# Convolution's means two iterations behind their power, the last gate's modulation fetched in pairs, the opening's blocks rounded ahead of the next columns

## The chip, the core and the metric

The kernel runs on one core of a Trainium2 chip, in one launch. The metric is the device time in microseconds; of several runs the median stands. The engines are TensorE (PE; its weight loads are listed apart as PEld), VectorE (DVE), ScalarE (ACT), GpSimd (POOL) and SyncE (SP), which issues most of the DMAs.

## What is computed

One encoder layer on x of 1024 x 1024 in float32, with three residual sub-layers: a SwiGLU FFN at half weight, a token mixer (a convolution group beside differential attention), and a second FFN. Each sub-layer is

```
shift, scale, gate = mod[:, 0], mod[:, 1], mod[:, 2]       # mod = silu(c) @ w_ada + b_ada, 9 x 1024 columns
y = f(x * (1 + scale) + shift)
x = layer_norm(ALPHA * x + weight * (1 + gate) * y, g, b)
```

The convolution group ends in a layer norm over its 512 channels and a silu. Only three places of this matter here: the modulation of the first sub-layer, with which everything begins; that layer norm's means; and the gate of the last sub-layer.

## The kernel before

Products are made in float32r: each operand is split into a rounded part (a copy on ScalarE, L143) and a remainder (a subtraction on VectorE, L144), and a product is three matmuls (high by high, high by low, low by high). The FFN's products follow a Strassen scheme with seven products per pair of column blocks.

The order of the instructions on an engine is not simply the written order: a planner fills each engine's queue ahead of the run, and `tc.issue_after(ins)` ties what is written inside it behind `ins`, in the queue of the engine of `ins` alone. A tied instruction doesn't wait for `ins` to end, it only stands behind it. Once made, the queues are fixed, and an engine that waits at one instruction holds up all behind it. Large temporary blocks come from one heap of 30 slots (`slot`, L64; `raw_slot`, L201).

**The opening** (`early`, L767, with `first_ada`, `first_x`, `first_mod`, `first_h`, L705 to L763). The shift and scale columns of the first sub-layer come in four chunks kk of 256 columns each. A chunk's modulation weights are four loads q of two slices each, so 8 slices j of 128 x 512. `first_mod` sums the first 6 slices on VectorE (L729, L731; NV is 3, and the loop runs to 2 n), lets TensorE sum the other two by matmuls with one output column (L737, 16 passes), and adds up the 128 partitions by further matmuls (L747). ScalarE makes the columns B0 and A0 from these (L744, L751). `first_h` transposes the chunk's x block on TensorE (L759) and applies scale and shift on ScalarE (L255). `right_first` (L258) then splits that block. What stands in `issue_after(columns)` is tied behind the last column sum of the chunk before, on TensorE; what stands in `issue_after(summed)` behind the last sum on VectorE. The split of block kk - 1 is written behind the columns of chunk kk. `in_gate` and `in_sums` prepare the first weights of the FFN: the first at kk = 1, the sums at kk = 3. After the opening, `mid` (L794) starts the products, tied behind the last columns on TensorE, and handles the second half of x (L811 is its first step on VectorE).

**The convolution's means** (`conv_stat`, L1243). After four blocks' statistics GpSimd makes the reciprocal root by a power (L1246, L1248); some steps later VectorE makes the negative mean times it (L1252) and ScalarE normalizes the four blocks (L1255). The steps are counted by `step(ST)`, called once in each of the 32 iterations of the attention loop with ST = 5; a `yield` uses one. `finish` (L1213) does the like for the attention's norm, with 2 ST yields between its power (L1217) and its use (L1220). Chains stand in one list, and a chain begins when the one ahead of it has ended.

**The last gate** (`ada_gate`, L187, called from `hook2`, L1471). `hook2(j)` is called after the products of column block j of the last FFN. At j = 10 and 13 it fetches four slices of two for one half of the gate (L166), which also sums them on VectorE (L155, L157), tied to nothing there; two iterations later the rest is written (one matmul, L194, and L196, L197). `pace["Y"]` is the last weight load issued, `pace["V"]` the last product on VectorE of an iteration (L480).

Of the kernel before, what the change touches and what calls it, by code (L numbers as in the profile page):

```python
# [1 line left out]

# [6 lines left out]
F32 = mybir.dt.float32  # L10
# [3 lines left out]
ALU = mybir.AluOpType  # L14
# [3 lines left out]
P = 128  # L18
T = 1024
NT = T // P  # L20
D = 1024
KD = D // P
# [3 lines left out]
H = 512  # L26
# [14 lines left out]
ST = 5  # L41
# [1 line left out]
CF = 3  # L43
AHEAD = 4
LATE = 0
NV = (3, 3, 3, 3)

# [1 line left out]
def layer_kernel(ctx, tc, a, out):  # L51
    nc = tc.nc
    V, S, G, PE, SY = nc.vector, nc.scalar, nc.gpsimd, nc.tensor, nc.sync
# [10 lines left out]
    def slot(name, shape=(P, 2, H), dt=F32R):  # L64
        return heap.tile(list(shape), dt, tag="h", bufs=HEAP, name=name)

    def bank(name, dt=F32):
        return psum.tile([P, H], dt, tag="ps", bufs=4, name=name)
# [78 lines left out]

    w_ada = a["w_ada"][0].rearrange("(p j) n -> p j n", j=KD)

    def ada_acc(raws, acc):  # L150
        n = 0
        for raw in raws:
            for jj in range(raw.shape[1]):
                if n == 0:
                    V.tensor_scalar(acc, raw[:, jj], c_act[:, 0:1], None, ALU.mult)  # L155
                else:
                    V.scalar_tensor_tensor(acc, raw[:, jj], c_act[:, n : n + 1], acc, ALU.mult, ALU.add)  # L157
                n += 1

    def ada_chunk(wp, take, s, m, half):  # L160
        col = (s * 3 + m) * D + half * H
        acc = wp.tile([P, H], F32, tag="ada_acc", bufs=1, name=f"ada{s}{m}{half}")
        raws = []
        for q in range(4):
            raw = take(f"adaw{s}{m}{half}{q}")
            SY.dma_start(raw, w_ada[:, 2 * q : 2 * q + 2, col : col + H])  # L166
            raws.append(raw)
        ada_acc(raws, acc)
        return acc

    mods = {}
# [12 lines left out]

        return rest

    def ada_gate(wp, take, s, w, g, half):  # L187
        if half == 0:
            SY.dma_start(g, a["b_ada"][:, (s * 3 + 2) * D : (s * 3 + 3) * D].partition_broadcast(P))
        acc = ada_chunk(wp, take, s, 2, half)  # L190

        def rest():
            ps = bank(f"adag{s}{half}")
            PE.matmul(ps, lhsT=ones, rhs=acc, start=True, stop=True)  # L194
            sl = g[:, half * H : (half + 1) * H]
            V.tensor_scalar(sl, sl, w, w, ALU.mult, ALU.add)  # L196
            V.scalar_tensor_tensor(sl, ps, w, sl, ALU.mult, ALU.add)  # L197

        return rest

    def raw_slot(name):  # L201
        return slot(name, dt=F32)
# [55 lines left out]
    def right_first(name, ops, hb, eng=V):  # L258

        hi, lo = slot(f"{name}bh"), slot(f"{name}bl")  # L260
        last = split(hi, lo, hb, eng)
        ops["B11"].append((hi[:, 0], lo[:, 0]))
        ops["B21"].append((hi[:, 1], lo[:, 1]))
        return last
# [114 lines left out]
    pace = {}  # L379
# [316 lines left out]
    with pool("p1a") as wp:  # L696
        in_tags(wp, "r4 ah al mw sh sl")
        ops = new_ops()
# [23 lines left out]
        def first_mod(kk, raws, n):  # L722

            ps = bank(f"ada0p{kk}")
            acc = slot(f"ada0a{kk}", (P, 2, 2, 256), F32)[:, 0]
            for j in range(2 * n):
                raw = raws[j // 2][:, j % 2]
                if j == 0:
                    V.tensor_scalar(acc, raw, c_act[:, 0:1], None, ALU.mult)  # L729
                else:  # L730
                    last = V.scalar_tensor_tensor(acc, raw, c_act[:, j : j + 1], acc, ALU.mult, ALU.add)  # L731
            part = small.tile([P, 4], F32, tag="part", bufs=2, name=f"part{kk}")
            two = bank(f"ada0q{kk}")
            for i in range(4):
                m, es, k = i // 2, slice(i % 2 * P, (i % 2 + 1) * P), 2 * kk + i % 2
                for j in range(2 * n, KD):
                    PE.matmul(  # L737
                        two[:, i : i + 1], lhsT=raws[j // 2][:, j % 2, m, es], rhs=c_act[:, j : j + 1],
                        start=j == 2 * n, stop=j == KD - 1,
                    )  # L740
            for i in range(4):
                k = 2 * kk + i % 2
                bias = (bcol(0, 0), bada1)[i // 2]
                S.activation(part[:, i : i + 1], two[:, i : i + 1], AF.Identity, bias=bias[:, k : k + 1], scale=1.0)  # L744
            for i in range(4):
                m, es = i // 2, slice(i % 2 * P, (i % 2 + 1) * P)
                pe = PE.matmul(ps[:, i : i + 1], lhsT=acc[:, m, es], rhs=ones[:, 0:1], start=True, stop=True)  # L747
            for i in range(4):
                k = 2 * kk + i % 2
                to = (B0, A0)[i // 2]  # L750
                S.activation(to[:, k : k + 1], ps[:, i : i + 1], AF.Identity, bias=part[:, i : i + 1], scale=1.0)  # L751
            return last.ins, pe.ins

        def first_h(kk, x, half):
            ps = wide(f"hT0_{kk}_{half}")
            for e in range(2):
                for i in range(4):
                    o = e * H + i * P
                    flipped[:] = [PE.transpose(ps[:, o : o + P], x[:, i, e * P : (e + 1) * P], ident).ins]  # L759
            h = slot(f"h0_{kk}_{half}", dt=F32)  # L760
            for e in range(2):
                h_of(h[:, e], ps[:, e * H : (e + 1) * H], A0, B0, 2 * kk + e)
            return h  # L763
# [3 lines left out]
        def early(wp, s, w_in, ops):  # L767

            with tc.issue_after(c_silu.ins):
                raws = [in_load(wp, s, w_in, 0, S)]  # L770
            ada, xb = [], []
            for kk in range(4):
                ada.append(first_ada(kk))
                xb.append(first_x(kk, 0))
            xc = [first_x(kk, 1) for kk in range(2)]
            raws.append(in_load(wp, s, w_in, 1))
            xc.extend(first_x(kk, 1) for kk in range(2, 4))
            hb, L = [], [{}, {}]
            for kk in range(4):
                with tc.issue_after(columns) if kk else nullcontext():  # L780
                    summed, columns = first_mod(kk, ada[kk], NV[kk])
                    hb.append(first_h(kk, xb[kk], 0))
                with tc.issue_after(summed):
                    if kk:
                        right_first(f"r0_{kk - 1}", ops, hb[kk - 1])
                    if kk == 1:
                        L[0].update(in_gate(wp, s, 0, raws[0]))
                    if kk == 3:
                        right_first("r0_3", ops, hb[3])
                        in_sums(wp, s, 0, raws[0], L[0])  # L790
            first.update(wp=wp, s=s, w_in=w_in, ops=ops, hb=hb, xc=xc, L=L, raws=raws, pe=columns)
            return L, ({}, {}), mid

# [176 lines left out]
    with pool("mproj") as wp:  # L970
        us, sig = [], []
        for i in range(4):
            ws = (pre, pre2)[i] if i < 2 else load_glu(wp, i, "whi", "wlo", 4, "raw", 3)
            q = quad(f"glu{i}", i % 2)
            for hs in ((0,), (1,)) if i == 0 else ((0, 1),):
                for k in range(KD):
                    wh, wl = (w[:, k % 4] for w in ws[k // 4])
                    for n, (w, x) in enumerate(((wh, 0), (wh, 1), (wl, 0))):
                        for m in range(2):
                            for h in hs:  # L980
                                PE.matmul(  # L981
                                    q[2 * m + h], lhsT=w[:, m * P : (m + 1) * P], rhs=hm[k][h][:, x],
                                    start=k == 0 and n == 0, stop=k == KD - 1 and n == 2,
# [177 lines left out]
    with pool("mattn") as wp:  # L1161
# [81 lines left out]
        def conv_stat(half):  # L1243
            mv = cstat[half]
            v = small.tile([P, 4], F32, tag="cv", bufs=2, name=f"cv{half}")
            G.tensor_scalar(v, mv[:, :, 1], 1.0, EPS, ALU.mult, ALU.add)  # L1246
            r = small.tile([P, 4], F32, tag="cr", bufs=2, name=f"cr{half}")
            G.tensor_tensor(r, v, mhalf, ALU.pow)  # L1248
            for _ in range(ST):
                yield  # L1250
            nm = small.tile([P, 4], F32, tag="cnm", bufs=2, name=f"cnm{half}")
            V.scalar_tensor_tensor(nm, mv[:, :, 0], -1.0, r, ALU.mult, ALU.mult)  # L1252
            for t in range(4):
                blk = cacc[:, :, (4 * half + t) * P : (4 * half + t + 1) * P]
                S.activation(blk, blk, AF.Identity, bias=nm[:, t : t + 1], scale=r[:, t : t + 1])  # L1255
            cstat[half] = None
# [53 lines left out]
    ops = new_ops()  # L1310
    hb, hc = [None] * 4, [None] * 4
    todo2 = {}
    TENG = (V, G)
    with pool("p3a") as wp:
# [3 lines left out]
        for t in range(NT):  # L1318
            tag = ("sf", "sf", "sh", "sl", "sh", "sl", "sh", "sl")[t]
# [118 lines left out]
        for c in range(len(groups)):  # L1438
            last = c == len(groups) - 1
            for t in range(5 if last else NT):  # L1440
# [9 lines left out]
                if c == 1 and t == 0:  # L1450
                    raws = [in_load(wp, 2, a["ffn2_w_in"][0], j) for j in range(2)]
# [19 lines left out]
        def hook2(j):  # L1471
            if 1 < j < NT + 2:
                residual_tile(j - 2)
            if j in (10, 13):
                if j == 10:
                    mods["gate2"] = rows.tile([P, D], F32, tag="gate1", name="gate2")
                with tc.issue_after(pace["Y"]):
                    todo2[j + 2] = ada_gate(wp, raw_slot, 2, 0.5, mods["gate2"], (j - 10) // 3)
            if j in todo2:
                todo2.pop(j)()  # L1480

        def early2(wp, s, w_in, ops):
            return left, ({}, {}), mid
# [73 lines left out]
```

## Time and profile before

| | |
|---|---|
| median of 3 runs | 1894.91 us (1892.62 to 1895.3) |
| the profiled execution | 1899.15 us |
| its span | 1897.4 us |
| instructions | 23451 |
| granted TensorE clock, mean over the span | 0.99 |
| DMA | 288.73 MB, 152 GB/s over the span |

All times in views are microseconds from the span's start. In a timeline row stand the start, the length, the engine, the line of the kernel, the operation, output and inputs with their shapes, the count of instructions that the row merges, and in brackets how long the engine idled before and what released it. A queue name such as SPq stands for the issuing of DMAs. In a table by windows the numbers behind each engine are its busy time and, in parentheses, its instructions.

### The profile page before, as it was taken

The page shows a single profiled execution, that of the slowest core. Times are in us where ns is not written, and L with a number is a line of the kernel's source. Part 1 is how long each engine was busy: PE and PEld are TensorE (multiplying, and loading weights), DVE is VectorE, ACT ScalarE, POOL GpSimd, SP SyncE. Part 2 cuts the span into 40 slices and gives each one's busy share as a digit, 9 for nine tenths or more (in the row PEclk, how much of TensorE's full clock was granted, in tenths as well). Part 3 has the DMA queues.
Part 4 walks back from the last instruction along what each step waited for, and adds up shares of the span by engine and source line. Part 5 has one row for each costly group of instructions (what it writes and reads, how often), then busy time and mean ns, then how long its engine had stood idle before and what let it go on. Part 6 is the DMA issues. An engine that isn't in the chain of part 4 may idle for free. (4 is left out here: it accounts for less than half of the span.)

```text
span 1897.4 us, 23451 instructions
## 1 busy us (share of the span) xinstructions
PE 1826.3 (96%) x8570; PEld 1513.1 (80%) x8570; DVE 1439.1 (76%) x1979; ACT 784.9 (41%) x1292; POOL 317.4 (17%) x322
## 2 busy tenths in 40 slices
PE   5999999999999999999999899979999999999997
PEld 5787888887888887887888788758887888888885
DVE  4988877897688777999676566587776665469888
ACT  2643333333445543122277781453332333354540
POOL 0001111011200011036467540350000000000011
PEclk9999999999999999999999999989999999999999
DMA  9268867785894323222000134125554433187432
GB/s 319 72 225 281 257 228 239 242 268 189 301 322 131 100 60 134 83 95 70 20 1 1 45 134 134 78 83 183 167 166 152 145 120 106 45 293 275 135 113 72
DMA packets 219378, 288.73 MB, mean 152 GB/s; under 512 B 15978, under 2 KB 126687, under 8 KB 219262
## 3 DMA queue, kind: packets, MB, share of 16 engines
q1 hardware_dynamic: 204842, 245.25, 39.9%
q0 software_dynamic: 11072, 38.80, 5.6%
q10 hardware_dynamic: 3348, 3.18, 0.5%
q8 instruction: 67, 1.10, 0.2%
q14 instruction: 49, 0.40, 0.1%
HBM read 209.06 MB, written 78.12 MB: 151 GB/s over the span
## 5 line engine op out<-in xcount | busy, mean ns | idle before, releaser
L587 PE MATMUL fo<-wr,gl 128*128 128x512 f32 x1848 | 421.5, 390 | 1.0 <-DVE pv L630 1.0
L587 PEld LDWEIGHTS fo<-wr,gl 128*128 128x128 f32 x1848 | 346.3, 188 | 74.1 <-DVE pv L630 1.4
L1000 DVE SCALAR_TENSOR_TENSOR cacc<-u,convw,cacc 128x1012 f32<-128x1012 f32 (+14 forms) x120 | 150.9, 1322 | 0.2
L144 DVE TENSOR_TENSOR gl<-gr,gl 128x512 fp32r<-128x512 f32 x148 | 101.4, 691 | 12.5 <-ACT gl L143 11.0
L143 ACT CAST gl<-gr 128x512 fp32r<-128x512 f32 x148 | 90.8, 618 | 26.3 <-DMA gr<-gd 19.4
L144 DVE TENSOR_TENSOR sl<-sf,sh 128x1024 fp32r<-128x1024 f32 x43 | 54.5, 1267 | 59.0 <-ACT sh L143 58.9
L1131 DVE TENSOR_REDUCE mx<-sc 128x1 f32<-128x1024 f32 x64 | 75.5, 1215 | 26.2 <-PE sc L1129 26.0
L219 POOL TENSOR_TENSOR rr<-rv,mhalf 128x1 f32<-128x1 f32 x24 | 22.2, 925 | 431.4 <-DVE rv L217 431.4
L157 DVE SCALAR_TENSOR_TENSOR ada<-adaw,c_act,ada 128x512 f32<-128x512 f32 x98 | 73.2, 747 | 25.3 <-DMA adaw<-in_w_ada_dram 24.8
L143 ACT CAST sh<-sf 128x1024 fp32r<-128x1024 f32 x44 | 46.4, 1054 | 104.8 <-PE fi_16S L373 5.8
L1133 ACT ACTIVATE p<-sc,mx 128x1024 f32<-128x1024 f32 x64 | 71.4, 1117 | 36.1 <-DVE mx L1131 36.0
L395 POOL DMA_DIRECT2D gd<-gf x8 | 4.4, 546 | 413.6 <-DVE gf L461 412.5
L423 ACT ACTIVATE gf<-gf 128x512 f32<-128x512 f32 x44 | 27.8, 632 | 106.0 <-DVE gf L422 103.0
L143 ACT CAST wr<-wa 128x512 fp32r<-128x512 f32 x66 | 41.2, 624 | 71.1 <-PE fo L587 70.1
L443 ACT ACTIVATE gf<-gf 128x512 f32<-128x512 f32 x44 | 27.7, 629 | 98.8 <-DVE gf L442 98.8
L981 PE MATMUL glu<-hm,gluh 128*128 128x512 f32 x256 | 65.6, 392 | 0.0
L1182 POOL TENSOR_TENSOR p<-p,p 128x1024 f32<-128x1024 f32 x27 | 64.2, 2377 | 1.5
L143 ACT CAST wr<-wb 128x512 fp32r<-128x512 f32 x66 | 40.2, 621 | 57.5 <-PE fo L587 40.4
L144 DVE TENSOR_TENSOR wr<-wa,wr 128x512 fp32r<-128x512 f32 x66 | 45.4, 687 | 24.0 <-ACT wr L143 23.7
L1199 PE MATMUL av<-vf,aT 128*128 128x128 f32 x512 | 62.4, 276 | 1.0 <-ACT cacc L1262 1.0
L144 DVE TENSOR_TENSOR sl<-r,sh 128x1024 fp32r<-128x1024 f32 x44 | 53.6, 1221 | 11.8 <-ACT sh L143 11.7
L1199 PEld LDWEIGHTS av<-vf,aT 128*128 128x128 f32 x512 | 59.7, 192 | 1.5 <-ACT cacc L1262 1.3
(3436 smaller groups left out, 4874.1 us busy)
## 6 DMA issues: line engine op xcount, KB each, us to landing
gr<-gd SPq DMA_DIRECT2D x148, 256.0 KB
adaw<-in_w_ada_dram SPq DMA_DIRECT2D x56, 512.0 KB
gd<-gf SPq DMA_DIRECT2D x102, 256.0 KB
r<-in_ffn_w_in_dram SPq DMA_DIRECT2D x84, 256.0 KB
ra<-in_ffn_w_in_dram SPq DMA_DIRECT2D x66, 256.0 KB
mwi<-mw POOLq DMA_DIRECT2D x24, 512.0 KB, 5.9
wb<-in_ffn_w_out_dram SPq DMA_DIRECT2D x44, 256.0 KB
wa<-in_ffn_w_out_dram SPq DMA_DIRECT2D x44, 256.0 KB
```

Of the source, the lines that this page charges most:

```text
L143: a = S.copy(hi, x)
L144: b = eng.tensor_tensor(lo, x, hi.bitcast(F32), ALU.subtract)
L157: V.scalar_tensor_tensor(acc, raw[:, jj], c_act[:, n : n + 1], acc, ALU.mult, ALU.add)
L423: S.activation(c0, c0, AF.Silu)
L443: pace["S"] = S.activation(c1, c1, AF.Silu).ins
L587: PE.matmul(ps, lhsT=g[:, x, ts_], rhs=w[:, y], start=n in (1, 2, 3) and k == i == 0, stop=k == NK - 1 and i == 2, skip_group_check=n not ...
L981: PE.matmul(q[2 * m + h], lhsT=w[:, m * P : (m + 1) * P], rhs=hm[k][h][:, x], start=k == 0 and n == 0, stop=k == KD - 1 and n == 2,)
L1000: V.scalar_tensor_tensor(acc[:, lo_t:hi_t], u[:, lo_t + sh : hi_t + sh], convw[:, i, jj : jj + 1], acc[:, lo_t:hi_t], ALU.mult, ALU.add,)
L1131: V.tensor_reduce(mx_, ps, axis=AX.X, op=ALU.max, negate=True)
L1133: S.activation(pe, ps, AF.Exp, bias=mx_, accum_out=sm[:, e : e + 1])
L1182: last = G.tensor_tensor(p0, p0, p1, ALU.add)
L1199: PE.matmul(ps[:, 0:P], lhsT=aT[:, kt], rhs=vf[kt][:, h * P : (h + 1) * P], start=kt == 0, stop=kt == 7)
```

## The change

NV becomes 7 and `first_mod` counts slices with it instead of pairs, so VectorE sums 7 of 8 slices and TensorE one. In the opening the rounding of a block (the copy on ScalarE) is written right behind its `first_h`, and what the next chunk has on ScalarE is tied behind it; the remainder on VectorE stays tied behind the sums of the next chunk. The first weights' split is written at kk = 0 instead of 1, and their sums are halved: order 0 at kk = 1, order 1 at kk = 3. In `conv_stat` L1252 and L1255 are written 2 ST steps behind the power instead of ST. The last gate becomes a generator that `hook2` steps from j = 10 to 17: it fetches two slices (at 10 and 14), sums them an iteration later behind the product on VectorE and fetches the other two, sums these another iteration later, and writes the rest one iteration after that.

```diff
-NV = (3, 3, 3, 3)
+NV = (7, 7, 7, 7)
...
-    def ada_acc(raws, acc):
-        n = 0
+    def ada_acc(raws, acc, n=0):
...
-    def ada_gate(wp, take, s, w, g, half):
+    def ada_gate(wp, take, s, w, g, half, staged=False):
...
+        def slow():
+
+            col = (s * 3 + 2) * D + half * H
+            acc = wp.tile([P, H], F32, tag="ada_acc", bufs=1, name=f"ada{s}2{half}")
+            raws = {}
+
+            def fetch(q):
+                raws[q] = take(f"adaw{s}2{half}{q}")
+                SY.dma_start(raws[q], w_ada[:, 2 * q : 2 * q + 2, col : col + H])
+
+            with tc.issue_after(pace["Y"]):
+                fetch(0)
+                fetch(1)
+            yield
+            for n in (0, 2):
+                with tc.issue_after(pace["V"]):
+                    for q in (n, n + 1):
+                        ada_acc([raws[q]], acc, 2 * q)
+                if n == 0:
+                    with tc.issue_after(pace["Y"]):
+                        fetch(2)
+                        fetch(3)
+                    yield
+            yield
+            rest(acc)
...
-            for j in range(2 * n):
+            for j in range(n):
...
-                for j in range(2 * n, KD):
+                for j in range(n, KD):
                     PE.matmul(
                         two[:, i : i + 1], lhsT=raws[j // 2][:, j % 2, m, es], rhs=c_act[:, j : j + 1],
-                        start=j == 2 * n, stop=j == KD - 1,
+                        start=j == n, stop=j == KD - 1,
                     )
...
+            def right_lo(kk):
+                lo = slot(f"r0_{kk}bl")
+                V.tensor_tensor(lo, hb[kk], hi[kk].bitcast(F32), ALU.subtract)
+                ops["B11"].append((hi[kk][:, 0], lo[:, 0]))
+                ops["B21"].append((hi[kk][:, 1], lo[:, 1]))
+
+            hi = []
             for kk in range(4):
-                with tc.issue_after(columns) if kk else nullcontext():
+                with ExitStack() as es:
+                    if kk:
+                        es.enter_context(tc.issue_after(columns))
+                        es.enter_context(tc.issue_after(rounded))
                     summed, columns = first_mod(kk, ada[kk], NV[kk])
                     hb.append(first_h(kk, xb[kk], 0))
+                    hi.append(slot(f"r0_{kk}bh"))
+                    rounded = S.copy(hi[kk], hb[kk]).ins
                 with tc.issue_after(summed):
                     if kk:
-                        right_first(f"r0_{kk - 1}", ops, hb[kk - 1])
-                    if kk == 1:
+                        right_lo(kk - 1)
+                    if kk == 0:
                         L[0].update(in_gate(wp, s, 0, raws[0]))
-                    if kk == 3:
-                        right_first("r0_3", ops, hb[3])
-                        in_sums(wp, s, 0, raws[0], L[0])
+                    elif kk == 1:
+                        in_sums(wp, s, 0, raws[0], L[0], order=(0,))
+                    elif kk == 3:
+                        right_lo(3)
+                        in_sums(wp, s, 0, raws[0], L[0], order=(1,))
...
-            for _ in range(ST):
+            for _ in range(2 * ST):
                 yield
...
-            if j in (10, 13):
+            if j in (10, 14):
...
-                    todo2[j + 2] = ada_gate(wp, raw_slot, 2, 0.5, mods["gate2"], (j - 10) // 3)
-            if j in todo2:
-                todo2.pop(j)()
+                    todo2["gate"] = ada_gate(wp, raw_slot, 2, 0.5, mods["gate2"], (j - 10) // 4, staged=True)
+            if 10 <= j <= 17:
+                next(todo2["gate"], None)
```

## Rows read from the trace of the kernel before

**Rows 1.** The page, part 1: busy time, share and instructions of each engine.
```profile
PE 1826.3 (96%) x8570; PEld 1513.1 (80%) x8570; DVE 1439.1 (76%) x1979; ACT 784.9 (41%) x1292; POOL 317.4 (17%) x322
```

**Rows 2.** Waits of TensorE over the span: total us, times, longest.
```profile
PE qTl L1113 <- DVE aT L1191: 4.8, 2, 2.5
...
PE fi_9A L373 <- DVE p L439: 2.4, 1, 2.4
```

**Rows 3.** Timeline of VectorE, opening: start, us, line, output, idle before.
```profile
32.04 1.23 DVE L144 TENSOR_TENSOR r_0bl<-h,r_0bh 128x1024 fp32r<-128x1024 f32 x1 [7.36 <-ACT r_0bh L143]
...
33.70 3.90 DVE L731 SCALAR_TENSOR_TENSOR ada0a<-ada,c_act,ada0a 128x512 f32<-128x512 f32 x5
42.64 1.23 DVE L144 TENSOR_TENSOR r_1bl<-h,r_1bh 128x1024 fp32r<-128x1024 f32 x1 [5.04 <-ACT r_1bh L143]
...
44.30 3.90 DVE L731 SCALAR_TENSOR_TENSOR ada0a<-ada,c_act,ada0a 128x512 f32<-128x512 f32 x5
...
57.78 1.29 DVE L811 TENSOR_TENSOR t<-h,h 128x512 f32<-128x512 f32 x2
```

**Rows 4.** Timeline of ScalarE, opening.
```profile
20.94 1.46 ACT L255 ACTIVATE h<-hT,B,A 128x512 f32<-128x512 f32 x2
...
30.96 1.05 ACT L143 CAST r_0bh<-h 128x1024 fp32r<-128x1024 f32 x1
...
50.52 0.41 ACT L751 ACTIVATE A<-ada0p,part 128x1 f32<-128x1 f32 x2
```

**Rows 5.** Timeline of TensorE, opening.
```profile
22.04 3.57 PE L737 MATMUL ada0q<-c_act,ada 128*128 128x1 f32 x16 [1.80 <-DMA ada<-in_w_ada_dram]
...
39.39 3.55 PE L737 MATMUL ada0q<-c_act,ada 128*128 128x1 f32 x16
42.80 1.95 PE L759 MATMUL hT<-ident,xc 128*128 128x128 f32 x8
48.25 1.87 PE L747 MATMUL ada0p<-ones,ada0a 128*128 128x1 f32 x8 [3.50 <-DVE ada0a L731]
```

**Rows 6.** Windows of the opening; the last three columns: granted clock, DMA share, GB/s.
```profile
20.00:40.00 20.00, 14.82 (x69) 14.28 (x69) 9.96 (x12) 6.85 (x24) 0.00 (x0) 1.00 1.09 348
...
50.00:60.00 10.00, 9.85 (x41) 7.84 (x42) 7.38 (x9) 9.33 (x16) 0.00 (x0) 1.00 0.10 26
```

**Rows 7.** Last gate: timelines of VectorE, SyncE, TensorE, then windows as in rows 6.
```profile
1427.92 0.42 DVE L196 TENSOR_SCALAR gate<-gate 128x512 f32<-128x512 f32 x1
...
1433.78 1.54 DVE L157 SCALAR_TENSOR_TENSOR ada<-adaw,c_act,ada 128x512 f32<-128x512 f32 x2 [3.52 <-DMA adaw<-in_w_ada_dram]
...
1475.44 1.23 DVE L144 TENSOR_TENSOR sl<-sf,sh 128x1024 fp32r<-128x1024 f32 x1 [5.55 <-ACT sh L143]
...
1494.48 1.22 DVE L144 TENSOR_TENSOR sl<-sf,sh 128x1024 fp32r<-128x1024 f32 x1 [4.96 <-ACT sh L143]
...
1428.03 0.37 SPq L166 DMA_DIRECT2D adaw<-in_w_ada_dram  x1
...
1439.97 0.50 PE L373 MATMUL fi_9A<-r_0t3h,ah 128*128 128x512 f32 x1 [2.38 <-DVE p L439]
...
1440.00:1442.00 2.00, 2.00 (x7) 1.66 (x8) 2.00 (x3) 0.63 (x1) 0.00 (x0) 0.79 0.45 131
1442.00:1444.00 2.00, 2.00 (x6) 1.52 (x6) 2.00 (x4) 0.00 (x0) 0.00 (x0) 0.50 0.15 54
1444.00:1446.00 2.00, 2.00 (x9) 1.60 (x8) 1.57 (x4) 1.48 (x1) 0.00 (x0) 0.85 0.56 208
```

**Rows 8.** Means: timelines of VectorE, GpSimd, TensorE, then waits from 1000 to 1200.
```profile
1086.44 0.16 DVE L1252 SCALAR_TENSOR_TENSOR cnm<-cmv,cr 128x4 f32<-128x4 f32 x1 [4.36 <-POOL cr L1248]
...
1085.38 1.02 POOL L1248 TENSOR_TENSOR cr<-cv,mhalf 128x4 f32<-128x4 f32 x1
...
1089.52 0.71 PE L1113 MATMUL qTl<-ident_r,ql 128*128 128x128 f32 x4 [2.49 <-DVE aT L1191]
...
DVE o L1220 <- POOL r L1217: 12.6, 6, 2.5
```

More of the change, by code (lines that the diff above doesn't have):

```diff
@@ L2 @@
-from contextlib import nullcontext
+from contextlib import ExitStack
 import concourse.bass as bass
@@ L185, in ada_cols, with rest @@
         return rest
-    def ada_gate(wp, take, s, w, g, half):
+    def ada_gate(wp, take, s, w, g, half, staged=False):
         if half == 0:
             SY.dma_start(g, a["b_ada"][:, (s * 3 + 2) * D : (s * 3 + 3) * D].partition_broadcast(P))
-        acc = ada_chunk(wp, take, s, 2, half)
-        def rest():
+        def slow():
[20 more added lines that the diff above has]
+            rest(acc)
+        acc0 = None if staged else ada_chunk(wp, take, s, 2, half)
+        def rest(acc=acc0):
             ps = bank(f"adag{s}{half}")
@@ L197, in rest @@
             V.scalar_tensor_tensor(sl, ps, w, sl, ALU.mult, ALU.add)
-        return rest
+        return slow() if staged else rest
     def raw_slot(name):
```

## The prediction

> **What bounds the kernel.** I read the page's busy shares first, then the waits of TensorE over the whole span, then the timelines of single engines at the three places that the diff touches, and the table by windows for the clock and the DMA rate. TensorE works 96% of the span [rows 1]; so only time in which it is held back can be won. Its waits outside the opening are few: one of 2.4 us in the second FFN and two of 2.4 us in the attention stage [rows 2]. In the opening it waits for data that is loading and then for sums on VectorE [rows 5]. The three edits lie at just these places.
>
> **The opening.** Modulation columns come in four chunks kk: VectorE sums 6 of 8 slices, TensorE takes the other two, a column sum gives scale and shift, ScalarE makes h, then rounds it, and VectorE takes the remainder. In the trace the remainder of chunk 0 holds VectorE for 7.36 us, because ScalarE rounds chunk 0 only at 30.96, behind h of chunk 1, although h of chunk 0 was done at 22.4; behind that remainder stand the sums of chunk 2. The same happens once more, for 5.04 us, ahead of the sums of chunk 3 [rows 3, 4]. So from chunk 2 on one chunk waits for the next in a ring: sums at 33.70 and again at 44.30, 10.6 us apart. The change rounds each block right behind its own h, ahead of the next chunk's columns on ScalarE, and so opens the ring; the remainder then finds its rounded block and the sums wait for their data alone.
>
> When is the data there? The last quarter of chunk 1 lands at 22.04, since TensorE waits for it until then [rows 5]. Up to the last quarter of chunk 3 there follow two x blocks of 0.52 MB and two chunks of 2.10 MB, 5.24 MB. The loads run at 348 GB/s [rows 6]: 15.1 us, so 37.1. From there TensorE needs, with 8 passes instead of 16, 3.55 / 2 = 1.8 us for the slice left to it, 1.95 us for the transposes (those of [rows 5] are the same eight), and 1.87 us for the column sums: 42.7. Before, the column sums ended at 48.25 + 1.87 = 50.1. VectorE is not late: after the landing it has one sum of 0.78 us (3.90 / 5) left. So the first products may start 7.4 us sooner. Behind them, ScalarE: before, it ended A at 50.9, 0.8 us after the columns; by that step and two more of 1.46 us and one of 1.05 us (h of chunk 3, its rounding, h of the second half) VectorE's next long series, L811, can start at about 47.4 instead of 57.78, 10.4 us sooner; the left blocks' sums (L341 to L345) and their remainders, which ran between the chunks' work and this series, now fall into VectorE's idle time. TensorE was 98% busy from 50 to 60 [rows 6], so its own 7.4 us is nearer to the truth than VectorE's 10.4, and a few short waits after 60 may shrink as VectorE is further ahead: I take 8.5 us.
> Added: one sum of 0.78 us per chunk on VectorE, 3.1 us in all, which its waits of 7.36 and 5.04 us cover; were that cover gone, and the ring still closed, the last three chunks would each be 0.78 us later, +2.3 us. Removed: 32 TensorE passes, beside the loads except in the last chunk. The bounds are therefore -10.4 and +2.3 us. The loads behind chunk 3 keep their order: by the same rate its x block lands at 38.6, before its transposes, and the first two blocks of the second half at 41.6, before 42.7; so nothing new is late there. The split of the first weights, now written a chunk earlier, may stand ahead of the sums of chunk 1, where VectorE waits for data anyway.
> A page would have it otherwise: the Trainium skill, "DMA: Bandwidth & Descriptors", section "Bandwidth", has a single core's 16 MB load at 425 GB/s. By it the last chunk would land at 34.4 and the opening would give some 2.6 us more, by estimate. The row of this case shows 348 GB/s over 20 us, so I don't use it.
>
> **The last gate.** Its sums are written for iteration 10, but nothing ties them there: a gate step written for iteration 15 runs at 1427.92, in iteration 9. The sums likewise come as soon as the first pair of slices has landed. Slots are short: the third slice is fetched at 1428.03, when the first sum has freed one, and VectorE then stands 3.52 us before the sums of the last slices. Behind it are queued the steps that read TensorE's banks, among them L439, and TensorE waits 2.38 us for that [rows 7]. After the wait the granted clock is 0.79, 0.50 and 0.85 in three windows of 2 us [rows 7]: 2 x (0.21 + 0.50 + 0.15) = 1.7 us more. Together 4.1 us. The change fetches two slices, ties their sums behind the product of the next iteration, an iteration later, 19.0 us by the cadence (1475.44 to 1494.48), and only then fetches two more. The third slice took under 6 us from its fetch to its sum (1428.03 to 1433.78), so no sum waits. What is queued behind the four sums (up to 4 x 0.77 = 3.1 us, from 1.54 for two) is L422 and the remainder next to it; behind it VectorE idles 5.55 and 4.96 us in two successive iterations [rows 7], and that idle time takes up the 3.1 us. Cost 0. Bounds: -4.1 us, and, if all four iterations with sums (11, 12, 15, 16) made TensorE wait as iteration 9 does, 4 x 4.1 - 4.1 = +12.3 us. I take -4.1: the row of the idle time is nearer.
>
> **The convolution's means.** In two places VectorE stands 4.36 us at L1252, which waits for the power on GpSimd; the power ends at 1086.40, because GpSimd has a long addition (L1182) ahead of it. Behind L1252 stand the maxima and a copy, and TensorE waits 2.49 us for the copy [rows 8]. With the same clock price as above, 2 x (2.5 + 1.7) = 8.4 us could be won if L1252 came behind them. The edit only writes L1252 five steps later. But the order on the engine isn't the written one: L1252 already runs before the maxima of an iteration that is written ahead of it, and L1220, which is written two iterations behind its power as L1252 will be, still waits for GpSimd in all its 6 places of the stage, 12.6 us in total [rows 8]. With the gate step above, six iterations early, I read this so: an instruction goes into its queue once its inputs are expected, wherever it was written, if nothing earlier is ready. Then five more steps move nothing. The other steps of the chains (and the last norm's, which end an iteration later) are written later too, and go early for the same reason. The blocks that L1255 makes are read again only behind the loop (`conv_back`). Bounds: -8.4 and 0, since nothing is added and nothing in the loop waits for a later L1252; I take 0.
>
> **The sum.** -8.5 - 4.1 + 0 = -12.6 us. The profiled execution took 1899.15 us (span 1897.4 and 1.75 around it): 1886.5. The median of the runs, 1894.91, is 4.2 us lower: 1882.3. All of it is carried to the end, as TensorE is full behind both places.
>
> **Rivals.**
> (a) The means move as well: 8.4 us more, 1873.9. For it speaks that L1220 stands behind the maxima, L1252 ahead of them; against it, that L1220 waits too. 0.17.
> (b) The opening wins less, because a step of the left block's sums comes into VectorE's queue ahead of the sums of chunk 2 and waits for a rounding that ScalarE makes only behind h and the rounding of chunk 1, at about 31.5. Remainder and sums (1.2 and 5.2 us) end at 37.9, the last chunk's remainder and sums at 44.3, the columns at 46.2: 3.9 us instead of 8.5. 1886.9. For it: VectorE's queue is fixed ahead, as [rows 3] show; against it: ScalarE is idle most of that time. 0.15.
> (c) The ring stays: the planned order still puts the remainder late, +2.3 - 4.1 = -1.8 us, 1893.1. Against it: the rounding is tied ahead of the next columns. 0.10.
> (d) Slower: the gate's sums, now tied behind L480 in four iterations, push the reading of TensorE's banks late, at +12.3 us, less the opening's 8.5: +3.8, 1898.7. It decides from the point where the sums and any wait for their slices exceed the 5 us that VectorE idles per iteration [rows 7]; with 3.1 us and 19 us of lead it shouldn't. 0.08.
> The forecast itself gets 0.50.
>
> **Numbers.** From no change this kernel's measurement can tell about 0.2%, 3.8 us. Forecast, (a) and (b) are faster by more: 0.82; (c) is within: 0.10; (d) is slower, by just that: 0.08. The range 1871 to 1891 holds the forecast, (a) and (b) with the opening's and the gate's own bounds, and leaves out (c) and (d).
>
> **What would show it.** Opening: no wait of VectorE for a rounded block over 1 us; the sums of chunk 3 end near 38, the first product starts near 42.7, L811 near 47.4. Rows with the sums of chunk 3 still near 44 show (b) or (c). Gate: no wait of VectorE for a slice after 1400, no wait of TensorE for L439 and no half clock there; a new wait in iterations 11, 12, 15 or 16 shows (d). Means: L1252 still right behind L1238 and waiting about 4.4 us; if it stands behind the maxima and TensorE's two waits are gone, (a). If the time is above 1891, the reading of the opening was wrong.

## The result, and the profile after

The changed kernel took 1882.14 us (median), the kernel before 1894.88 beside it: ratio 0.9931, 95% interval 0.9912 to 0.9951, 13.1 us. One of the four runs, of 2600.95 us at a mean granted clock of 0.66, is in that median but not in the ratio; the other three took 1880.01 to 1883.73 us, with 1880.56 in the middle. The forecast was 1882.3. Timed once more (e5 below), it gave 1882.21 us, ratio 0.992 (0.9906 to 0.9934), 15.2 us. The total is right, but partly by luck: of its three terms two were wrong, in opposite directions, as the traces show.

Busy time of the changed kernel, the page's first part; it answers to [rows 1]:
```profile
PE 1814.1 (97%) x8538; PEld 1505.4 (80%) x8538; DVE 1442.2 (77%) x1983; ACT 784.6 (42%) x1292; POOL 319.2 (17%) x322
```
TensorE has 32 passes fewer, 12.2 us less busy time, and again no slack. Its waits over the span (total, times, longest), the rows that answer to [rows 2]:
```profile
PE qTl L1152 <- DVE aT L1230: 2.6, 2, 2.3
```
That wait is down from 4.8 us, and the one for L439 has no row any more.

Timeline of VectorE in the opening of the changed kernel (start, duration, line, output and inputs; in brackets the idle time before and who ended it), answering to [rows 3]:
```profile
25.88 1.22 DVE L806 TENSOR_TENSOR r_0bl<-h,r_0bh 128x1024 fp32r<-128x1024 f32 x1
31.03 1.23 DVE L144 TENSOR_TENSOR sl<-r,sh 128x1024 fp32r<-128x1024 f32 x1 [3.93 <-ACT sh L143]
32.17 0.48 DVE L754 TENSOR_SCALAR ada0a<-ada,c_act 128x512 f32<-128x512 f32 x1
32.69 4.69 DVE L756 SCALAR_TENSOR_TENSOR ada0a<-ada,c_act,ada0a 128x512 f32<-128x512 f32 x6
37.29 1.22 DVE L806 TENSOR_TENSOR r_1bl<-h,r_1bh 128x1024 fp32r<-128x1024 f32 x1
...
38.95 4.69 DVE L756 SCALAR_TENSOR_TENSOR ada0a<-ada,c_act,ada0a 128x512 f32<-128x512 f32 x6
...
51.89 0.69 DVE L850 TENSOR_TENSOR t<-h,h 128x512 f32<-128x512 f32 x1
```
ScalarE there, answering to [rows 4], and TensorE, answering to [rows 5]:
```profile
22.58 1.05 ACT L819 CAST r_0bh<-h 128x1024 fp32r<-128x1024 f32 x1
...
28.61 1.45 ACT L280 ACTIVATE h<-hT,B,A 128x512 f32<-128x512 f32 x2
29.95 1.05 ACT L143 CAST sh<-r 128x1024 fp32r<-128x1024 f32 x1
30.88 1.06 ACT L819 CAST r_1bh<-h 128x1024 fp32r<-128x1024 f32 x1
```
```profile
37.43 1.87 PE L772 MATMUL ada0p<-ones,ada0a 128*128 128x1 f32 x8 [3.42 <-DVE ada0a L756]
...
43.69 1.87 PE L772 MATMUL ada0p<-ones,ada0a 128*128 128x1 f32 x8 [0.87 <-DVE ada0a L756]
45.41 0.77 PE L398 MATMUL fi_0A<-r_0bh,ah 128*128 128x512 f32 x1
```
The remainders r_0bl and r_1bl no longer wait: the ring is open, each block is rounded right behind its h. (r_3bl still waits 4.25 us, but behind the last sums.) But another step now stands ahead of the sums of chunk 2: sl, the remainder of the first left block. Its rounded half sh is made behind h of chunk 1, at 29.95, and VectorE stands 3.93 us. This is rival (b) in its place; only the rounding of chunk 1, at 30.88, comes behind sh and not ahead of it. What it costs lies between the forecast and the rival: chunk 3's sums end at 43.64 (forecast near 38, rival (b) 44.3), the first product starts at 45.41 (42.7 and 46.2), the series that was L811 and is L850 at 51.89 (forecast 47.4). The loads run as before [rows 6]; two windows of the changed kernel:
```profile
20.00:30.00 10.00, 5.91 (x27) 5.68 (x28) 6.88 (x9) 5.81 (x18) 0.00 (x0) 1.00 1.09 348
30.00:40.00 10.00, 6.16 (x28) 5.71 (x29) 8.69 (x12) 3.16 (x12) 0.00 (x0) 1.00 1.09 348
```

The last gate, answering to [rows 7]: VectorE's two longest waits from 1400 to 1600 (total, times, longest), then VectorE, SyncE, and windows (the last three columns: granted clock, DMA share, GB/s):
```profile
DVE sl L144 <- ACT sh L143: 51.6, 22, 5.6
DVE gf L447 <- issue: 4.8, 4, 2.0
```
```profile
1484.45 0.75 DVE L156 SCALAR_TENSOR_TENSOR ada<-adaw,c_act,ada 128x512 f32<-128x512 f32 x1
...
1468.40 0.38 SPq L197 DMA_DIRECT2D adaw<-in_w_ada_dram  x1
...
1420.00:1424.00 4.00, 4.00 (x20) 3.30 (x19) 2.53 (x5) 0.69 (x1) 0.00 (x0) 1.00 0.24 70
1424.00:1428.00 4.00, 4.00 (x19) 3.34 (x18) 3.78 (x7) 2.38 (x3) 0.00 (x0) 1.00 0.18 66
```
The third slice is fetched at 1468.40 and summed at 1484.45, without a wait; no wait for a slice is left in the stretch, TensorE's for L439 is gone, and the clock stays at 1.00 (2.4 GHz). All as forecast.

The means, answering to [rows 8]: VectorE at both places, then TensorE behind each:
```profile
1047.05 0.16 DVE L1291 SCALAR_TENSOR_TENSOR cnm<-cmv,cr 128x4 f32<-128x4 f32 x1 [4.36 <-POOL cr L1287]
...
1073.55 2.36 DVE L1170 TENSOR_REDUCE mx<-sc 128x1 f32<-128x1024 f32 x2 [0.77 <-PE sc L1168]
1076.99 0.16 DVE L1291 SCALAR_TENSOR_TENSOR cnm<-cmv,cr 128x4 f32<-128x4 f32 x1 [1.09 <-POOL cr L1287]
```
```profile
1050.14 0.53 PE L1152 MATMUL qTl<-ident_r,ql 128*128 128x128 f32 x4 [2.34 <-DVE aT L1230]
...
1077.81 0.87 PE L1152 MATMUL qTl<-ident_r,ql 128*128 128x128 f32 x8 [0.28 <-DVE aT L1230]
```
The first mean stands where it stood; so does L1220, now L1259, which waits 12.8 us in 6 places (12.6 before). The second has moved behind the maxima, and TensorE's wait there fell from 2.49 us to 0.28: half of rival (a).

**Stage by stage.** Each trace is one execution, and equal stages differ between traces. So the same matmul is looked up in all of them: its start, or the time between two. (They are named by the times of the kernel before; where one has no record, the nearest that has, moved by the difference.) o: the opening changed, m: the means, M: both means tied, g: the gate, l: left block late, 6: six sums; in brackets, a part of such an edit alone. The runs e1 to e12 are told below.
```
                  first     the one   the one   1000 to   1420 to
                  product   at 66.5   at 880    1140      1500
before    -        50.0      66.5      880.0     140.0     80.0
e2        g        50.1      66.4      877.0     141.1     75.7
e3        m        49.6      66.2      879.6     136.7     78.0
e4        (m)      49.8      66.5      877.2     140.3     76.9
e9        (g)      50.5      67.4      878.8     141.0     75.7
e10       (g)      50.4      66.9      880.6     139.8     79.7
e11       m        50.1      66.0      879.7     138.5     81.7
e1        o        45.1      59.3      871.8     141.0     79.3
changed   o m g    45.4      60.1      869.4     137.9     75.6
e5        o m g    45.1      60.1      871.9     136.6     75.7
e7        o M g    45.0      59.7      872.0     132.9     75.7
e6        o l m g  42.9      58.4      868.7     137.6     75.7
e8        o l M g  42.6      58.1      868.1     133.0     75.6
e12       o6l M g  44.2      59.8      876.3     133.0     75.7
```
Means over the groups: the opening brings 4.9 us at the first product (50.07 to 45.15, e1, changed, e5, e7), 6.8 at 66.5 and 7.7 at 880 (878.99 to 871.28). The means bring 3.1 us (140.53 to 137.46, e4 counted with the unchanged), the gate 3.6 (79.27 to 75.69, e10 counted with the unchanged, as its stall is still there). The opening's figure is the least certain: read at other matmuls between 200 and 880 the same groups lie 7.1 to 8.0 us apart, because single traces lose 1 to 2 us in places; at 820 it is 7.1, and the rest of the 7.7 is a fall of the clock near 870, at a place that no edit touches (last section). Together 14.4 us (13.8 with the opening read at 820), between the two timed differences of 13.1 and 15.2. The first two profiles alone differ by 18.6 us: the profiled execution of the kernel before was 4.2 us above its median.

### The profile page after: what moved, and what is told of

The parts are those of the page before. It is cut to its first block, busy times and chain, and to the rows that moved or that the text cites. A ratio compares the mean times of both kernels' runs of the same rounds, so it can differ in the third digit from the quotient of the medians.

```text
span 1878.8 us, 23393 instructions
## 1 busy us (share of the span) xinstructions
PE 1814.1 (97%) x8538; PEld 1505.4 (80%) x8538; DVE 1442.2 (77%) x1983; ACT 784.6 (42%) x1292; POOL 319.2 (17%) x322
## 5 line engine op out<-in xcount | busy, mean ns | idle before, releaser
L144 DVE TENSOR_TENSOR gl<-gr,gl 128x512 fp32r<-128x512 f32 x148 | 101.8, 694 | 15.3 <-ACT gl L143 13.8
```

What stands on the lines that cost most here:

```text
L144: b = eng.tensor_tensor(lo, x, hi.bitcast(F32), ALU.subtract)
```

## Experiments

All ratios are against the kernel before, timed beside each run.

**e1, e2, e3: one part of the change each.** Each is the kernel before with the hunks of one part: `NV`, the rounding in the loop, `right_lo` and `in_sums` by halves (e1); `ada_gate` with `staged` and `hook2` (e2); `2 * ST` in `conv_stat` (e3).

> Only the opening's part of the change; gate and means as before. Theory of the prediction (ring opened, the sums wait for their data alone): first product starts near 42.7, gain 8.5 us, 1886.4. Theory read from the trace after (rival b: the first step of the left block's split, sl, stands ahead of the sums of chunk 2 and waits for its rounding behind h of chunk 1): a wait of about 3.9 us at L144 for sh near 27 to 31, sums of chunk 3 end at 43.6, first product at 45.4, 4.6 us sooner; gain 4.6 to 6.3 us, 1888.6 to 1890.3. If more than 8.5 us come out all the same, VectorE's lead in the first FFN gives the rest.

Measured 1888.02 us, ratio 0.9949 (0.9929 to 0.9968). The trace has the same wait for sh, and the first product at 45.11: the second theory, up to there. The whole, 7.7 us by the table's groups and 9.7 by the times, is more than its 4.6 to 6.3: what follows gains too. The interval of the times, 6.1 to 13.5 us, would by itself still allow 6.3.

> Only the last gate's part of the change. Prediction: the wait of 2.4 us and the half clock behind it go, no new wait comes: gain 4.1 us, 1890.8. Rival d (four iterations with sums each hold TensorE up): slower by up to 12.3 us, with waits of TensorE between 1440 and 1560. Rival: the wait was only a symptom and TensorE waits as long elsewhere: no gain.

1891.56 us, 0.9972 (0.996 to 0.9984): 5.3 us, the interval 3.0 to 7.6 holds the forecast 4.1. No new wait; rival (d) is out.

> Only the convolution's part of the change: the scaled mean written five steps later for both halves. Prediction: nothing moves, both stay right behind the statistics, gain 0 (1894.9). Theory from the trace after: the second of the two stands behind the two maxima, its wait of 4.4 us shrinks to about 1, and TensorE's wait of 2.5 us behind it goes with the half clock after it: gain 2 to 4.2 us, 1890.7 to 1892.9; the first stays and waits 4.4 us as before.

1892.33 us, 0.9974 (0.9962 to 0.9986): 4.9 us, 3.8 by the table's row (140.5 to 136.7). The forecast's zero is refuted. VectorE at the second place in e3:
```profile
1085.96 0.16 DVE L1252 SCALAR_TENSOR_TENSOR cnm<-cmv,cr 128x4 f32<-128x4 f32 x1 [1.10 <-POOL cr L1248]
```

**e4 and e11: five more steps for one half alone**, `range(2 * ST if half == 1 else ST)` (e4) and `half == 0` (e11). The question is why the second mean moved and the first didn't.

> Five steps more for the second half's mean alone. Theory 1 (its own later place in the text moves it): as with both halves, the second stands behind the maxima, gain 2 to 4.2 us. Theory 2 (the steps of the chains are taken from one list, one chain at a time; it was the first half's longer chain that put everything behind it an iteration later, the second half's power too): nothing moves, both waits of 4.4 us stay, gain 0.

> The counterpart of e4: five steps more for the first half's mean alone. Theory 2 of e4 (one chain at a time: the first half's longer chain puts the second half's statistics behind it, its power too, an iteration later): the second mean stands behind the maxima, as with both halves, TensorE's wait of 2.5 us there goes; gain 3.4 us in the trace from 1075 to 1125, about 4.9 us as in e3. Theory 1 (the second mean's own place moves it): gain 0.

VectorE at the second place, in e4 and then in e11:
```profile
1083.63 0.17 DVE L1252 SCALAR_TENSOR_TENSOR cnm<-cmv,cr 128x4 f32<-128x4 f32 x1 [4.38 <-POOL cr L1248]
```
```profile
1087.35 0.16 DVE L1252 SCALAR_TENSOR_TENSOR cnm<-cmv,cr 128x4 f32<-128x4 f32 x1 [1.08 <-POOL cr L1248]
```
With its own steps lengthened the second mean stays (e4); with only the first's lengthened it moves (e11). Theory 2 holds: `step` advances only the chain at the head of its list, so a longer first chain lets the ones behind it begin later, and the second half's power, with which its chain begins, is written later too. Its mean then comes behind the maxima. Counting the yields of the list gives the same: the second half's power is written in iteration 24 before and in e4, in 25 in e3 and e11. On the chip the power still ends where it did (at 1086.40 before, at 1085.93 in e3); what has moved is the mean's place on VectorE. The mean's own place in the text moved nothing, for either half. The stretch from 1075 to 1125 takes 50.3 us in e4, 47.1 in e11 and 45.9 in e3. The times alone would not have told it: both ratios are 0.9987 (e4 0.9973 to 1.0001, e11 0.9976 to 0.9998). e4, where nothing moved, is 2.5 us below too, with an interval that holds zero; so some of e3's 4.9 us may be chance.

**e5 to e8: the two waits that were left.** e6, beside the changed kernel:
```diff
-                    elif kk == 1:
-                        in_sums(wp, s, 0, raws[0], L[0], order=(0,))
                     elif kk == 3:
                         right_lo(3)
-                        in_sums(wp, s, 0, raws[0], L[0], order=(1,))
+                        in_sums(wp, s, 0, raws[0], L[0], order=(0, 1))
```
e7, where `mxs` keeps the last maximum's instruction:
```diff
-            V.scalar_tensor_tensor(nm, mv[:, :, 0], -1.0, r, ALU.mult, ALU.mult)
+            with tc.issue_after(mxs[-1]):
+                V.scalar_tensor_tensor(nm, mv[:, :, 0], -1.0, r, ALU.mult, ALU.mult)
```

> The changed kernel once more, beside the three below on one chip. If the parts add up (opening, gate and means alone gave ratios of 0.9949, 0.9972 and 0.9974), 0.9895 or 19.9 us; if the parts' gains hold something of the kernel before that is not there in each run (its wait of 2.4 us in the last gate was 0.9 to 2.0 us in three runs with that part unchanged, once with and twice without a half clock behind it), about 0.993 as it was timed first, 13 us.

> The changed kernel with the sums and the split of the first left block behind the sums of the last chunk of columns, where they were in the kernel before. Theory (rival b): the split's wait of 3.9 us for its rounding held the sums of chunk 2 and so those of chunk 3; without it chunk 3's sums end near 38, the first product starts near 42.7 instead of 45.4 and L850 near 50 instead of 51.9: 2 to 3 us less than the changed kernel. Rival: the data bound the sums anyway, or the later split makes the first S products late: no gain, or up to 2 us more.

> The changed kernel with the scaled mean tied behind the last maximum written before it, in both halves. Theory: the first of the two leaves its place right behind the statistics, VectorE's wait of 4.4 us there goes and so does TensorE's of 2.3 us: 2.3 to 4 us less than the changed kernel (the larger if the half clock goes too). Rival: VectorE then waits as long for the next thing from GpSimd, and TensorE behind it: no gain.

> e6 and e7 together. If both theories hold, 4.3 to 7 us less than the changed kernel; if neither, the same as that.

| run | median us | lowest to highest | ratio, interval |
|---|---|---|---|
| e5 | 1882.21 | 1881.81 to 1883.57 | 0.992, 0.9906 to 0.9934 |
| e6 | 1882.41 | 1879.06 to 1882.63 | 0.992, 0.9906 to 0.9933 |
| e7 | 1878.71 | 1877.96 to 1880.25 | 0.9901, 0.9887 to 0.9915 |
| e8 | 1876.89 | 1875.03 to 1878.61 | 0.989, 0.9876 to 0.9905 |

e5 leaves out 0.9895, the sum of the parts: 19.9 us were timed for the parts singly, 15.2 together; each part's interval is wide enough for its share of the difference, and the three were set against the same runs of the kernel before, so that an error in those counts three times. The other theory's 13 us lie inside e5's interval (12.5 to 17.8).

The opening of e6, VectorE, then TensorE:
```profile
26.50 0.75 DVE L756 SCALAR_TENSOR_TENSOR ada0a<-ada,c_act,ada0a 128x512 f32<-128x512 f32 x1
27.51 3.90 DVE L756 SCALAR_TENSOR_TENSOR ada0a<-ada,c_act,ada0a 128x512 f32<-128x512 f32 x5 [0.26 <-DMA ada<-in_w_ada_dram]
...
35.04 3.90 DVE L756 SCALAR_TENSOR_TENSOR ada0a<-ada,c_act,ada0a 128x512 f32<-128x512 f32 x5 [0.23 <-DMA ada<-in_w_ada_dram]
```
```profile
37.31 1.84 PE L762 MATMUL ada0q<-c_act,ada 128*128 128x1 f32 x8 [1.82 <-DMA ada<-in_w_ada_dram]
39.58 1.94 PE L784 MATMUL hT<-ident,xc 128*128 128x128 f32 x8 [0.43 <-ACT part L769]
41.31 1.71 PE L772 MATMUL ada0p<-ones,ada0a 128*128 128x1 f32 x8
42.87 0.78 PE L398 MATMUL fi_0A<-r_0bh,ah 128*128 128x512 f32 x1
```
Without sl in the way VectorE's sums wait for data alone, and the first product starts at 42.87, where the prediction had put it for the change itself (42.7). The last quarter of the columns landed by 37.31, forecast 37.1. By the 425 GB/s of the Trainium skill, "DMA: Bandwidth & Descriptors", section "Bandwidth", it would by estimate have landed at 34.4; this run disagrees. At 880 the two runs with l lie 2.9 us ahead of the four with o alone (1.6 at 200, 1.9 at 400). In the time e8 is below e7 by 1.8 us, but e6 is not below e5: that the 2.9 us reach the end is not shown by the medians of e5 and e6.

e7 is faster than e5: all its runs lie below all of e5's. From 1000 to 1140 it is 3.7 us shorter (136.6 to 132.9); with the second half's gain that makes 7.6 us against the means unchanged, close to the 8.4 that rival (a) had. At the matmul that e5 starts at 1091.56 it was even 7.3 us ahead; then TensorE waited where it hadn't, in e7:
```profile
1093.08 0.66 PE L276 MATMUL aT<-ident,p 128*128 128x128 f32 x4 [1.10 <-POOL p L1221]
...
1101.10 1.09 PE L276 MATMUL aT<-ident,p 128*128 128x128 f32 x8 [1.00 <-POOL p L1221]
...
1105.65 0.66 PE L276 MATMUL aT<-ident,p 128*128 128x128 f32 x4 [1.23 <-DVE aT L1230]
```
GpSimd's addition ends last at the first two. At the third it is a copy on VectorE, and it comes late because a step ahead of it took 3.23 us beside another such addition; VectorE and GpSimd in e7:
```profile
1098.89 3.23 DVE L1218 SCALAR_TENSOR_TENSOR p<-p,c,p 128x1024 f32<-128x1024 f32 x1
1098.67 2.38 POOL L1221 TENSOR_TENSOR p<-p,p 128x1024 f32<-128x1024 f32 x1
```
In the changed kernel this step takes 1.28 us, with no addition of GpSimd beside it; e7's second mean too took 1.58 us beside an addition, against 0.16. e8 and e12 show the same lengths. That the two engines hold each other up is how these rows read; no run tests it. By 1109 the lead is 3.6 us: half of what the tie wins is given back. e8 is the fastest version measured.

**e9 and e10: which half of the gate's edit counts.** e9 is the kernel before with `tc.issue_after(pace["V"])` around its unstaged `ada_gate` call in `hook2`; e10 is e2 without that tie around the sums.

> The kernel before, with only the tie of the last gate's sums behind the product of an iteration, without the fetching in pairs: all eight sums of a half stand in one iteration (11, then 14), the third and fourth slice are fetched when the first sums free their slots. Theory 1 (it is the pairs that count: slices fetched an iteration ahead of their sums): VectorE stands 2.5 to 3.5 us for the third slice as before, TensorE waits 0.9 to 2.4 us behind it: gain 0 to 1.5 us. Theory 2 (the later place is enough, VectorE idles 5 us per iteration there): no wait of TensorE, gain as with the pairs, 2 to 5 us.

> The gate's part of the change alone, without the ties of the sums: slices fetched in pairs, but the sums of both pairs stand in VectorE's queue one behind the other, in iteration 9 or 10 for the first half, ahead of the iteration in which the second pair is fetched. Theory (the tie is needed with the pairs): VectorE stands for the second pair until SyncE has come to its fetch, up to an iteration (19 us), and TensorE behind it: 5 to 30 us slower than the kernel before, in two places. Rival: the second pair's fetch comes early as well: as with the ties, 2 to 5 us faster.

e9: 1893.0 us, 0.998 (0.9969 to 0.9991). e10: 1896.47 us, 1.0 (0.999 to 1.0011). VectorE in e9, then VectorE, SyncE and TensorE in e10:
```profile
1465.70 1.54 DVE L157 SCALAR_TENSOR_TENSOR ada<-adaw,c_act,ada 128x512 f32<-128x512 f32 x2 [1.24 <-DMA adaw<-in_w_ada_dram]
1468.37 1.54 DVE L157 SCALAR_TENSOR_TENSOR ada<-adaw,c_act,ada 128x512 f32<-128x512 f32 x2 [1.13 <-DMA adaw<-in_w_ada_dram]
```
```profile
1434.28 3.11 DVE L156 SCALAR_TENSOR_TENSOR ada<-adaw,c_act,ada 128x512 f32<-128x512 f32 x4 [5.07 <-DMA adaw<-in_w_ada_dram]
...
1428.03 1.58 SPq L197 DMA_DIRECT2D adaw<-in_w_ada_dram  x2
...
1439.91 0.50 PE L397 MATMUL fi_9A<-r_0t3h,ah 128*128 128x512 f32 x1 [2.08 <-DVE p L463]
```
The later place is enough: e9's sums still wait 1.24 and 1.13 us for slices, but where VectorE has room, and its stretch is as short as with the pairs (75.7). The times, 3.8 us here and 5.3 in e2, do not tell the two apart. The pairs without the tie win nothing, and theory 1 of e9 is out. The expectation for e10 missed the size: the second pair was fetched at 1428.03, not an iteration later (its tie to the loads allows that; why it went so early was not tested); VectorE stood 5.07 us, not 19.

**e12: six sums again**, `NV = (6, 6, 6, 6)` in e8.

> The version of e8 with six sums on VectorE and two slices for TensorE, as the kernel before had them, instead of seven and one. Theory: once the sums wait for data alone, TensorE's own passes stand behind the last landing, 3.55 us instead of 1.84, while VectorE's last sum (0.78 us) was beside them: first product at 44.6 instead of 42.9, 1.7 us slower than e8. Rival: VectorE's sums are what ends last there even now: up to 0.8 us faster than e8.

TensorE in e12:
```profile
37.53 3.54 PE L762 MATMUL ada0q<-c_act,ada 128*128 128x1 f32 x16 [0.67 <-ACT A L776]
...
44.23 0.77 PE L398 MATMUL fi_0A<-r_0bh,ah 128*128 128x512 f32 x1
```
First product at 44.23, 1.6 us behind e8 (42.59), as the theory had it (1.7). The time, 1878.49 us with 0.9914 (0.9898 to 0.9929), lies 1.6 us above e8's; the intervals overlap, so the whole is unclear. Of the 7.5 us that e8's first product wins (from 50.07, the mean of the unchanged openings), 5.8 are the new order's and 1.6 the seventh sum's. The profiled runs are further apart than the medians, as e12's is the slowest of its six and e8's the fastest of its four: e12's trace loses 6.6 us more by 880, 5.1 of it in small waits for ScalarE and VectorE in the first FFN (1.1 us at most) that e8's doesn't have, 1.5 by the clock near 865.

## Why the prediction came out right

- **The opening, 8.5 us: it gave 7.7, by another way.** The step that failed: "the left blocks' sums (L341 to L345) and their remainders ... now fall into VectorE's idle time". One remainder made idle time instead, 3.93 us ahead of the sums of chunk 2. The forecast held that the sums "wait for their data alone"; they do in e6, and its first product lies within 0.2 us of the forecast. So the landing, the 8 passes and the chain behind them were sized rightly, and the order on VectorE wasn't read to its end. The first product won 4.9 instead of 7.4 us. Rival (b) had the place, and the columns' end to 0.6 us (43.69 + 1.87 = 45.6 against 46.2), but stopped there: 2.8 us more came behind the first product, where the series on VectorE starts 5.9 us sooner (57.78 to 51.89). For that the forecast had taken 1.1.
- **The gate, 4.1 us: 3.6 by the table, 5.3 timed; the mechanism as written, but for the pairs, which e9 does without.** One of its two terms, the clock's 1.7 us, was a matter of chance: see the last section.
- **The means, 0: 3.1 us.** The step that failed: "Then five more steps move nothing." For the instruction that was looked at, L1252, it is true (e4, and the first half in all runs without the tie of e7). But the steps are those of a list with one chain at a time, and the text noted only that the other chains "go early for the same reason". They don't: a chain's first instructions can't be written before the chain ahead of it has ended.
- **The sum.** 7.7 + 3.6 + 3.1 = 14.4 against 12.6. The opening and the gate came out 0.8 and 0.5 us smaller, the means 3.1 larger; 1.8 us is left, inside the spread of the two timings. That the forecast and the median agree to 0.2 us is luck: two errors offset each other, and the runs spread by more than that. Rival (a) came true for one half of two, rival (b) in its mechanism; (c) and (d) not at all.
- **What bounds the kernel.** The count of TensorE's waits outside the opening was short. The same view of the kernel before has five more of 1.9 to 2.9 us, between 1229 and 1273 at the start of the second FFN, 10.7 us together. The change doesn't touch that place, so the sum did not suffer; four of the five are still above 1.7 us in the changed kernel.

## What to carry to other kernels

When an edit adds a delay to a step of a work list, ask what the list holds behind it: the delay may do nothing for its own step and move another. When a wait is removed from an engine's queue, list what the same edit now puts into that queue, and when each item's input is made; here 3.93 of 7.36 us came back as the wait of a step whose result is first used at 58.53. A burst of side work is cheapest tied to a place where its engine idles; whether its data then came singly or in pairs made no difference to the stretch here.

## What the hardware showed that was not expected

Six traces have the gate's stall (in e10 with the slices in pairs), and TensorE's wait there differs: 0.90 (e4), 1.78 (e1), 2.00 (e3), 2.08 (e10), 2.38 (before) and 2.99 us (e11). So does what follows. Behind the 2.00 us in e3, and behind the 2.99 us in e11, windows of 2 us:
```profile
1435.70:1437.70 2.00, 2.00 (x9) 1.66 (x10) 2.00 (x3) 0.63 (x1) 0.00 (x0) 1.00 0.48 131
```
```profile
1437.30:1439.30 2.00, 1.98 (x5) 1.59 (x6) 2.00 (x3) 0.63 (x1) 0.00 (x0) 0.50 0.48 131
1439.30:1441.30 2.00, 2.00 (x6) 1.55 (x5) 2.00 (x4) 0.00 (x0) 0.00 (x0) 0.50 0.11 42
1441.30:1443.30 2.00, 2.00 (x6) 1.58 (x5) 0.56 (x2) 0.88 (x1) 0.00 (x0) 0.50 0.59 220
```
After 2.00 us the clock stayed at 2.4 GHz, after 1.78 us in e1 it fell to 0.73 and 0.50, after 2.99 to 0.50 (1.2 GHz) for three windows, 2 x 1.5 = 3 us lost. The length of the wait alone doesn't decide it. A place that no edit touched shows it better: near 870 TensorE waits 1.09 to 1.16 us for khl, a remainder that VectorE makes, in all fourteen traces. Behind that the granted clock fell to 0.50 to 0.54 at its lowest in four of them (before, e3, e11, e12), which cost some 1.5 us; in the other ten it stayed at 1.00. TensorE and a window behind it in the kernel before, then in e9, whose wait is the longest of all:
```profile
868.69 0.28 PE L1071 MATMUL kT<-ident_r,khl 128*128 128x128 f32 x1 [1.15 <-DVE khl L144]
870.69:872.69 2.00, 2.00 (x7) 1.62 (x7) 2.00 (x2) 1.39 (x6) 0.00 (x0) 0.62 0.00 0
```
```profile
869.14 0.28 PE L1071 MATMUL kT<-ident_r,khl 128*128 128x128 f32 x1 [1.16 <-DVE khl L144]
871.14:873.14 2.00, 2.00 (x10) 1.66 (x10) 2.00 (x2) 1.39 (x6) 0.00 (x0) 1.00 0.00 0
```
The Trainium skill, "TensorE: Matmul & The Clock Gate", section "Part 1: The HAM clock gate", has the point at which the clock rises depend on where a kernel's first matmul falls in a window that runs on by itself. It says so of the rise; these rows would fit the same for the fall, which no run here tests. At the gate, one and the same stall cost between 0.9 and 6.0 us; the stretch from 1420 to 1500 took 76.9 to 81.7 us with it, and 75.6 or 75.7 in all eight runs without. What one profile shows as the price of a stall is one draw, and removing it also removes the spread.
